# One scheduling context for both parts of a two-layer encoder trunk, with the latents kept in SBUF

## The chip, the cores and the metric

The kernel runs on one core of a Trainium2 chip. The metric is the device time of one execution in microseconds. The five engines are named as in the profile: PE (TensorE, with PEld for its weight loads), DVE (VectorE), ACT (ScalarE), POOL (GpSimd) and SP (SyncE, which here only issues DMAs). All numbers are 32 bit; each large matrix product is made of three matmuls over operands that are split into a high part and a low part.

## The reference

1024 tokens of width 1024 get 16 learned meta tokens in front (1040 in all) and pass two layers. The first is a gated linear attention, the second a latent attention whose keys and values come from a compressed latent. What matters here is the seam between them:

```python
# layer A ends:  h = x + (rms_norm(o) * silu(gate)) @ w_out
c = rms_norm(h, g) @ w_down                      # 256 latent + 64 rotary columns
c_kv = rms_norm(c[..., :256], g_latent)          # "ckv"
k_nope, v = c_kv @ w_uk, c_kv @ w_uv             # 8 heads x 128 each
# layer B, queries and gate:
z = rms_norm(h, g_b) @ w_in
c_q = rms_norm(z[..., :384], g_q_latent)         # "cq"
gate = z[..., 384:]                              # 1024 columns
q = rms_norm(c_q @ w_uq)                         # 8 heads x (128 + 64 rotary)
o = attention(q, k, v) * silu(gate)              # causal by chunks of 64
out = h + o @ w_out
```

## The kernel before, in words

`kernel` opens two tile contexts, one after the other, and each is scheduled by itself. `body` (L117) makes layer A, then the latents and the gates of layer B; `body2` (L961) makes the attention and the last projection. Within a context the scheduler orders the instructions of each engine by a simulation, and each engine then runs its own list in that order. The first context is planned by the plainer of two simulations, the second by the more detailed one. The engines all finish the first context before the second one starts.

The end of `body`: `latent_kv` (L878) and `latent_q` (L906) make the latents tile by tile in SBUF, transposed and split (`ckvT`, `cqT`), with the rotary key `kpe`, the sums `ssk` and the tables `qC`, `qS`. L934 to L938 write all of these to DRAM: the two latents on POOL's queue, the rest on SP's. Then the loop at L943 makes the gates, head by head: `load_wg` (L830) loads 512 KB of weights through SP and splits them (high part on POOL at L101, low part on DVE at L102); 48 matmuls fill two PSUM banks; ACT applies SiLU; SP stores the head's rows to DRAM (`gb_scr`, L954). The first head's weights (`wg0`) have a place of their own, so they are ready early; the others take turns in two buffers, which lie where the latents' weights `wd_hi` to `wq_lo` were.

The start of `body2`: POOL makes an identity matrix. `pair_weights(0, ...)` (L985) loads the up-projection weights of the first two heads (`uk`, `uv`, `uq`) and splits them, the high part on ACT (L1000) and the low part on DVE (L1001). `load(0, 1)` reads the first 256 tokens' latents (with the meta tokens) back from DRAM on POOL's queue, and SP reads the small tables. Constants such as `hide` and `qr_lo` are set on DVE. Then `build` makes one unit: keys, values and queries of 256 tokens for a pair of heads. Its first matmuls are the `uk` projection of `ckvT` (written to a bank of the tag `bd`), whose copy `kk` is squared on ACT, scaled on DVE, turned on PE, split again and used by `scores`. The remaining latents come with `load(1, NU)` (L1409).

The main loop (L1411) goes over 4 pairs of heads and 4 units each; `weave` mixes the scores of one unit with the build of the next and the weighing of the last. When the last unit is built, the pool `lcT` (latents and pair weights) is closed and the output weights `wf_hi`, `wf_lo` take its place (L1427 to L1438); `out_b` (L1443) then makes the output rows.

The order of two pools matters below. In `body` the PSUM pool `psB` (L752) has five banks for the tag `sc`, from which the gates take theirs in turn; in `body2` the pool `psB2` (L972) begins with the three banks of `bd`.

Of the kernel before, what the change touches and what calls it, by code (L numbers as in the profile page):

```python
# [28 lines left out]
NT = T // P  # L29
# [7 lines left out]
ROPE = 64  # L37
QK = NOPE + ROPE
# [10 lines left out]
def tools(tc):  # L49

    nc = tc.nc
    V, A, G, TE = nc.vector, nc.scalar, nc.gpsimd, nc.tensor
    uid = next(PART)
    number = [0]

    def tpool(**k):
        return tc.tile_pool(reuse_waits="tile", **k)

    def nm(s):
        number[0] += 1  # L60
        return f"{s}_{uid}_{number[0]}"

    NOSYNC = mybir.DependencyInfo(mybir.DependencyClass.NoSync, mybir.DependencyReason.DATA)
    tab = {"set": None, "before": [], "now": []}

    def act(out_ap, in_ap, func, **kw):

        want = {AF.Exp: "le", AF.Ln: "le", AF.Silu: "silu"}.get(func)

        def behind(i, others):  # L70
            for o in others:
                tc.add_manual_dep(i.ins, o.name, NOSYNC, reason="table order")

        new = want is not None and want != tab["set"]
        if new:
            tab["set"] = want
            tab["before"], tab["now"] = tab["now"], []
            if want == "le":
                i = A.preload_act_table_set("natural_log_exp_and_others")
                behind(i, tab["before"])  # L80
                tab["before"] = [i.ins]
        i = A.activation(out_ap, in_ap, func, **kw)  # L82
        if want is not None:
            behind(i, tab["before"])
            tab["now"].append(i.ins)
            if new and want != "le":
                tab["before"] = [i.ins]
        return i

    def mm3(ps, ahi, alo, bhi, blo, first, last):  # L90
        TE.matmul(ps, ahi, bhi, start=first, stop=False)  # L91
        TE.matmul(ps, ahi, blo, start=False, stop=False)  # L92
        TE.matmul(ps, alo, bhi, start=False, stop=last)  # L93

    def split_w(raw, hi, lo, gain=None, eng=G):

        if gain is None:
            eng.tensor_scalar(out=hi, in0=raw, scalar1=1.0, scalar2=1.0, op0=ALU.mult, op1=ALU.mult)  # L98
            V.tensor_tensor(out=lo, in0=raw, in1=hi, op=ALU.subtract)  # L99
        else:  # L100
            G.tensor_scalar(out=hi, in0=raw, scalar1=gain, scalar2=1.0, op0=ALU.mult, op1=ALU.mult)  # L101
            return V.scalar_tensor_tensor(out=lo, in0=raw, scalar=gain, in1=hi, op0=ALU.mult, op1=ALU.subtract)  # L102

    def split_ps(ps, hi, lo, gain=None):

        if gain is None:
            A.copy(hi, ps)  # L107
            V.tensor_tensor(out=lo, in0=ps, in1=hi, op=ALU.subtract)  # L108
        else:
            A.mul(hi, ps, gain)  # L110
            V.scalar_tensor_tensor(out=lo, in0=ps, scalar=gain, in1=hi, op0=ALU.mult, op1=ALU.subtract)

    return tpool, nm, act, mm3, split_w, split_ps


@with_exitstack
def body(ctx: ExitStack, tc: tile.TileContext, I):  # L117

    nc = tc.nc
    V, A, G, TE, SY = nc.vector, nc.scalar, nc.gpsimd, nc.tensor, nc.sync  # L120
    tpool, nm, act, mm3, split_w, split_ps = tools(tc)
# [14 lines left out]
    cp = ctx.enter_context(tpool(name="const", bufs=1))  # L136
# [612 lines left out]
        gathered = {t: out_gather(t, bank) for t in (-1, 0)}  # L749


    ps_b = ctx.enter_context(tpool(name="psB", bufs=2, space=PSUM))  # L752

    def bank2(tag, shape):
        tag = {"mm": "sc", "tr": "bd", "tb": "pt"}.get(tag, tag)
# [2 lines left out]
    with ExitStack() as lb:  # L758
# [172 lines left out]
                    wg0 = load_wg(lpre.enter_context(tpool(name="wg0", bufs=1, side="right")), 0)  # L931


        st = {}  # L934
        for key, y in (("ckvT", ckvT), ("cqT", cqT), ("kpe", kpe), ("ssk", ssk), ("qC", qC), ("qS", qS), ("gg", gg)):
            st[key] = nc.dram_tensor(key + "_scr", y.shape, F32R if "T" in key else F32).ap()
            (G if "T" in key else SY).dma_start(st[key], y)
        st.update(gb_scr=gb_scr, ot_scr=ot_scr, x1_scr=x1_scr)  # L938


        with ExitStack() as lg:
            wg = lg.enter_context(tpool(name="wg", bufs=2))
            for h in range(H):  # L943
                hi, lo = wg0 if h == 0 else load_wg(wg, h)
                z = wg.tile([P, T], F32, tag="z", name=nm("z"))
                for half in range(2):
                    c = slice(512 * half, 512 * half + 512)
                    cc = slice(NM + 512 * half, NM + 512 * half + 512)
                    ps = bank2("mm", [P, 512])
                    for kt in range(KT):  # L950
                        mm3(ps, hi[:, kt, :], lo[:, kt, :], h1_hi[:, kt, cc], h1_lo[:, kt, cc],
                            kt == 0, kt == KT - 1)
                    act(z[:, c], ps, AF.Silu)
                SY.dma_start(gb_scr[h * P:(h + 1) * P, :], z)  # L954
        lpre.close()

    return st


@with_exitstack  # L960
def body2(ctx: ExitStack, tc: tile.TileContext, I, out, st):  # L961

    nc = tc.nc
    V, A, G, TE, SY = nc.vector, nc.scalar, nc.gpsimd, nc.tensor, nc.sync
    tpool, nm, act, mm3, split_w, split_ps = tools(tc)

    cp = ctx.enter_context(tpool(name="const2", bufs=1))
    ident = cp.tile([P, P], F32, name="ident2")
    make_identity(nc, ident)
    gg = cp.tile([P, 1], F32, name="gg2")  # L970
    gb_scr, ot_scr, x1_scr = st["gb_scr"], st["ot_scr"], st["x1_scr"]
# [5 lines left out]
    lcT = ctx.enter_context(ExitStack())  # L977
    cpool = lcT.enter_context(tpool(name="cT2", bufs=1))

    wt = lcT.enter_context(tpool(name="wt", bufs=1))  # L980
    w_uk = I["kv_w_uk"].rearrange("(kt p) c -> p kt c", p=P)
    w_uv = I["kv_w_uv"].rearrange("(kt p) c -> p kt c", p=P)
    w_uq = I["b_w_uq"][0].rearrange("(kt p) c -> p kt c", p=P)

    def pair_weights(p, out_):  # L985

        h0 = 2 * p
        srcs = ((w_uk[:, :, h0 * P:(h0 + 2) * P], 2, 256, "uk"), (w_uv[:, :, h0 * P:(h0 + 2) * P], 2, 256, "uv"),
                (w_uq[:, :, h0 * QK:(h0 + 2) * QK], 3, 2 * QK, "uq"))
        raws = []  # L990

        for src, kts, w, _ in srcs:
            raws.append(wt.tile([P, 3, 2 * QK], F32, tag="raw", name=nm("raw"), bufs=3)[:, 0:kts, 0:w])
            SY.dma_start(raws[-1], src)
        yield 300
        for i, (_, kts, w, tag) in enumerate(srcs):
            hi = wt.tile([P, kts, w], F32R, tag=tag + "h", name=nm(tag))
            lo = wt.tile([P, kts, w], F32R, tag=tag + "l", name=nm(tag))
            if p == 0:
                A.copy(hi, raws[i])  # L1000
                V.tensor_tensor(out=lo, in0=raws[i], in1=hi, op=ALU.subtract)  # L1001
            else:
                split_w(raws[i], hi, lo)
            out_ += [hi, lo]
            yield 300

    wts = {0: []}
    w0 = pair_weights(0, wts[0])
    next(w0)
    ckvT = cpool.tile([P, 2, 2, L], F32R, name="ckvT2")  # L1010
    cqT = cpool.tile([P, 2, 3, T], F32R, name="cqT2")
    ckvT_hi, ckvT_lo, cqT_hi, cqT_lo = ckvT[:, 0], ckvT[:, 1], cqT[:, 0], cqT[:, 1]
    kpe = cpool.tile([P, NT + 1, ROPE], F32, name="kpe2")
    ssk = cpool.tile([P, NT + 1], F32, name="ssk2")
    qC, qS = (cpool.tile([P, NT, ROPE], F32, name=x) for x in ("qC2", "qS2"))

    def load(u0, u1):

        a, b = (0 if u0 == 0 else NM + 256 * u0), NM + 256 * u1
        four = lambda x: x.rearrange("p y j n -> p (y j) n")  # L1020
        G.dma_start(four(ckvT)[:, :, a:b], four(st["ckvT"])[:, :, a:b])
        a, b = 256 * u0, 256 * u1
        G.dma_start(four(cqT)[:, :, a:b], four(st["cqT"])[:, :, a:b])

    load(0, 1)
    for x, y in ((ssk, "ssk"), (kpe, "kpe"), (gg, "gg"), (qC, "qC"), (qS, "qS")):
        SY.dma_start(x, st[y])
    for _ in w0:
        pass


    lf = ctx.enter_context(ExitStack())
    with ExitStack() as lt:
# [372 lines left out]
        bd_t = lambda g: 7300 + (2000 if g == 0 else 0)  # L1406

        weave((started(0), 1, 0, 1))
        load(1, NU)  # L1409
        last, lt_ = None, 1  # L1410
        for n, (p, g) in enumerate(seq):  # L1411
            us = [units[p, u] for u in range(g + 1)]
# [88 lines left out]
```

## Time and profile before

| what | value |
|---|---|
| median of 3 runs | 1375.03 us (1369.99 to 1378.83) |
| profiled execution, its own time | 1379.86 us |
| its span, first to last instruction | 1378.0 us |
| mean granted TensorE clock | 0.978 |
| PE busy | 1320.7 us (96%) |
| DVE, ACT, POOL busy | 901.3, 541.7, 411.8 us |

The profile covers one execution. Its span is 1.86 us shorter than its device time, and its device time is 4.83 us above the median of the runs. A term that is read from the trace is taken off that execution, and the same difference is then taken off the median. A granted clock of 1.00 means 2.4 GHz and 0.50 means 1.2 GHz. Idle time of an engine is written in brackets in a timeline row, with what ended it.

### The profile page before, as it was taken

What the parts mean: (1) busy time and instruction counts of PE and PEld (TensorE: products, weight loads), DVE (VectorE), ACT (ScalarE), POOL (GpSimd) and SP (SyncE); (2) the same over time, 40 slices, a digit from 0 to 9 for tenths busy, and PEclk for the clock granted to TensorE, in tenths of its full rate; (3) what the DMA queues carried; (4) which work ended last, traced back from release to release, by engine and by line L of the source; (5) the groups of instructions that cost most, each with busy time, mean ns of one, the idle gap of its engine ahead of it and who ended that gap; (6) DMA issues with size and microseconds to landing.
All of it is one profiled execution on the core that took longest, in us unless ns stands there. A gap on an engine that the chain in (4) does not pass through costs nothing. (4 is left out here: it accounts for less than half of the span.)

```text
span 1378.0 us, 25002 instructions
## 1 busy us (share of the span) xinstructions
PE 1320.7 (96%) x9064; PEld 1191.2 (86%) x9064; DVE 901.3 (65%) x2625; ACT 541.7 (39%) x1709; POOL 411.8 (30%) x689
## 2 busy tenths in 40 slices
PE   6999999999999999999999999995999999998998
PEld 4879989988997999897788798884899999998787
DVE  5669778968986895544554764214887878878321
ACT  6442333233323431211222243114777777776200
POOL 3344224314332130041011402212454545347100
PEclk9999999999998999999999999997999999999999
DMA  5211202121211213136542306318010101004443
GB/s 175 46 25 47 51 20 65 32 50 40 53 42 24 54 39 92 51 96 222 166 141 79 108 1 224 108 46 265 25 49 28 61 24 33 24 32 135 129 147 118
DMA packets 121276, 109.01 MB, mean 79 GB/s; under 512 B 29230, under 2 KB 108142, under 8 KB 120898
## 3 DMA queue, kind: packets, MB, share of 16 engines
q1 hardware_dynamic: 118242, 96.88, 23.6%
q0 software_dynamic: 2912, 10.55, 2.1%
q8 instruction: 71, 1.16, 0.4%
q14 instruction: 51, 0.42, 0.1%
HBM read 74.29 MB, written 33.11 MB: 78 GB/s over the span
## 5 line engine op out<-in xcount | busy, mean ns | idle before, releaser
L91 PE MATMUL mm<-hT_hi,whi 128*128 128x384 f32 (+1 forms) x768 | 258.8, 337 | 2.6 <-DVE whi L98 2.5
L93 PE MATMUL mm<-hT_hi,wlo 128*128 128x384 f32 (+1 forms) x768 | 257.5, 335 | 0.4 <-DVE wlo L99 0.4
L92 PE MATMUL mm<-hT_lo,whi 128*128 128x384 f32 (+1 forms) x768 | 256.8, 334 | 0.0
L91 PEld LDWEIGHTS mm<-hT_hi,whi 128*128 128x128 f32 x768 | 148.4, 193 | 4.4 <-issue 3.2
L93 PEld LDWEIGHTS mm<-hT_hi,wlo 128*128 128x128 f32 x768 | 148.3, 193 | 3.2 <-DVE wlo L99 0.9
L92 PEld LDWEIGHTS mm<-hT_lo,whi 128*128 128x128 f32 x768 | 148.5, 193 | 1.3 <-issue 0.8
L108 DVE TENSOR_TENSOR pTl<-pt,pTh 128x256 fp32r<-128x256 f32 (+2 forms) x112 | 55.0, 494 | 14.1 <-ACT pTh L107 12.7
L98 POOL TENSOR_SCALAR whi<-raw 128x512 fp32r<-128x512 f32 x48 | 39.0, 826 | 73.6 <-PE mm L92 66.8
L82 ACT ACTIVATE P<-P,mx 128x144 f32<-128x144 f32 (+3 forms) x64 | 50.6, 791 | 21.2 <-DVE mx L1298 13.2
L91 PE MATMUL sc<-wo_hi,oTh 128*128 128x512 f32 (+1 forms) x144 | 57.5, 399 | 0.6 <-issue 0.6
L371 ACT COPY z<-mm 128x384 f32<-128x384 f32 (+1 forms) x72 | 31.9, 443 | 65.0 <-PE mm L93 64.8
L93 PE MATMUL sc<-wo_hi,oTl 128*128 128x512 f32 (+1 forms) x144 | 57.2, 397 | 0.0
L92 PE MATMUL sc<-wo_lo,oTh 128*128 128x512 f32 (+1 forms) x144 | 56.9, 395 | 0.0
L376 DVE SCALAR_TENSOR_TENSOR kn<-z,pcol,kn 128x384 f32<-128x384 f32 (+1 forms) x72 | 42.4, 589 | 18.3 <-POOL kn L373 17.4
L99 DVE TENSOR_TENSOR wlo<-raw,whi 128x512 fp32r<-128x512 f32 x64 | 47.3, 745 | 10.7 <-POOL whi L98 10.4
L102 DVE SCALAR_TENSOR_TENSOR wlo<-raw,pcol,whi 128x128 fp32r<-128x128 f32 x64 | 23.2, 419 | 46.2 <-POOL whi L101 46.2
L107 ACT CAST pTh<-pt 128x256 fp32r<-128x256 f32 (+2 forms) x112 | 47.2, 427 | 12.5 <-DVE pTl L108 8.6
L1311 POOL TENSOR_SCALAR P<-P,sl 128x144 f32<-128x144 f32 (+3 forms) x64 | 49.8, 778 | 4.2
L1309 POOL TENSOR_SCALAR Pe<-P,sl 128x128 f32<-128x128 f32 x64 | 27.1, 423 | 80.2 <-DVE sl L1306 55.1
L93 PE MATMUL sc<-h_hi,wlo 128*128 128x512 f32 x128 | 50.8, 397 | 0.0
L91 PE MATMUL bd<-wf_hi,oTh 128*128 128x512 f32 x128 | 50.0, 390 | 0.9 <-ACT oTh L1451 0.9
L91 PE MATMUL sc<-kn_hi,qn_hi 128*128 128x272 f32 (+3 forms) x160 | 48.4, 304 | 2.4 <-DVE mx L1298 1.9
(390 smaller groups left out, 4005.4 us busy)
## 6 DMA issues: line engine op xcount, KB each, us to landing
raw<-in_a_w_in SPq DMA_DIRECT2D x64, 256.0 KB
xt<-in_x SPq DMA_DIRECT2D x16, 512.0 KB
o_scr<-o SPq DMA_DIRECT2D x64, 64.0 KB
raw<-in_a_w_out SPq DMA_DIRECT2D x8, 512.0 KB
on<-o_scr SPq DMA_DIRECT2D x8, 512.0 KB
x_scr<-xt SPq DMA_DIRECT2D x8, 512.0 KB
raw<-in_b_w_in SPq DMA_DIRECT2D x8, 512.0 KB
gb_scr<-z SPq DMA_DIRECT2D x8, 512.0 KB
```

The lines of the kernel that those rows point to most:

```text
L82: i = A.activation(out_ap, in_ap, func, **kw)
L91: TE.matmul(ps, ahi, bhi, start=first, stop=False)
L92: TE.matmul(ps, ahi, blo, start=False, stop=False)
L93: TE.matmul(ps, alo, bhi, start=False, stop=last)
L98: eng.tensor_scalar(out=hi, in0=raw, scalar1=1.0, scalar2=1.0, op0=ALU.mult, op1=ALU.mult)
L99: V.tensor_tensor(out=lo, in0=raw, in1=hi, op=ALU.subtract)
L107: A.copy(hi, ps)
L108: V.tensor_tensor(out=lo, in0=ps, in1=hi, op=ALU.subtract)
L371: A.copy(z[:, 3 + a:3 + b], gemm_T(hi, lo, c))
L376: V.scalar_tensor_tensor(out=yc, in0=z[:, a + j:b + j], scalar=col("cw", 24 * j + m), in1=yc, op0=ALU.mult, op1=ALU.add)
L1309: G.tensor_scalar(out=Pe, in0=Pm[:, None, 0:NM].broadcast_to([P, E8, NM]), scalar1=s, scalar2=1.0, op0=ALU.mult, op1=ALU.mult)
L1311: G.tensor_scalar(out=Pm[:, 0:n], in0=Pm[:, 0:n], scalar1=s, scalar2=1.0, op0=ALU.mult, op1=ALU.mult)
```

## The change

There is one context. `body` goes on into what was `body2`, which becomes a block of it: a block is scheduled as a unit, nothing traced before it is placed among its instructions, and it is planned by the detailed simulation while the rest keeps the plain one. The latents, `kpe`, `ssk`, `qC`, `qS` and `gg` are not written to DRAM and read back; the attention reads the tiles that the latents were made in. The second identity matrix goes. The first pair's weights get tiles in a pool `wt` that is opened ahead of the gates, in the place right behind the latents; their loads are issued ahead of the gates' loop, and one step of their split is taken after the gate of each head from the third on, on POOL and DVE (it was ACT and DVE). The raw tiles have a size of their own for each of the three weights, where three of the largest size took turns.

```diff
-        st = {}
-        for key, y in (("ckvT", ckvT), ("cqT", cqT), ("kpe", kpe), ("ssk", ssk), ("qC", qC), ("qS", qS), ("gg", gg)):
-            st[key] = nc.dram_tensor(key + "_scr", y.shape, F32R if "T" in key else F32).ap()
-            (G if "T" in key else SY).dma_start(st[key], y)
+        wt = lcT.enter_context(tpool(name="wt", bufs=1))
...
+        wtiles = {}
+        for kts, w, tag in ((2, 256, "uk"), (2, 256, "uv"), (3, 2 * QK, "uq")):
+            wtiles[tag] = [wt.tile([P, kts, w], dt, name=tag + y) for y, dt in (("r", F32), ("h", F32R), ("l", F32R))]
+        def pair_weights(p, out_):
...
+            for src, kts, w, tag in srcs:
+                SY.dma_start(wtiles[tag][0], src)
+            yield 300
+            for i, (_, kts, w, tag) in enumerate(srcs):
+                raw, hi, lo = wtiles[tag]
+                split_w(raw, hi, lo)
+                out_ += [hi, lo]
+                yield 300
+        wts = {0: []}
+        w0 = pair_weights(0, wts[0])
+        next(w0)
...
                 SY.dma_start(gb_scr[h * P:(h + 1) * P, :], z)
+                if h > 1:
+                    next(w0, None)
         lpre.close()
-    return st
-def body2(ctx: ExitStack, tc: tile.TileContext, I, out, st):
...
-    ident = cp.tile([P, P], F32, name="ident2")
-    make_identity(nc, ident)
+    lps.close()
+    ctx.enter_context(tc.block(schedule_with_timeline_sim=True))
...
-            if p == 0:
-                A.copy(hi, raws[i])
-                V.tensor_tensor(out=lo, in0=raws[i], in1=hi, op=ALU.subtract)
-            else:
-                split_w(raws[i], hi, lo)
...
-        G.dma_start(four(ckvT)[:, :, a:b], four(st["ckvT"])[:, :, a:b])
...
-        G.dma_start(four(cqT)[:, :, a:b], four(st["cqT"])[:, :, a:b])
-    load(0, 1)
-    for x, y in ((ssk, "ssk"), (kpe, "kpe"), (gg, "gg"), (qC, "qC"), (qS, "qS")):
-        SY.dma_start(x, st[y])
...
-        load(1, NU)
...
-    with tile.TileContext(nc) as tc:
-        st = body(tc, I)
-    with tile.TileContext(nc, schedule_with_timeline_sim=True) as tc:
-        body2(tc, I, out, st)
+    with tile.TileContext(nc, schedule_with_timeline_sim=False) as tc:
+        body(tc, I, out)
```

## Rows read from the trace of the kernel before

**Rows 1.** Page, busy time, share of the span and instructions of each engine.

```profile
PE 1320.7 (96%) x9064; PEld 1191.2 (86%) x9064; DVE 901.3 (65%) x2625; ACT 541.7 (39%) x1709; POOL 411.8 (30%) x689
```

**Rows 2.** Stretches: length, busy us (instructions) of PE, PEld, DVE, ACT, POOL, clock, DMA.

```profile
920.00:930.00 10.00, 10.00 (x45) 8.06 (x44) 0.00 (x0) 1.20 (x2) 0.00 (x0) 1.00 0.13 52
...
931.70:945.10 13.40, 0.01 (x2) 0.04 (x1) 3.85 (x14) 3.45 (x5) 3.70 (x6) 0.67 0.78 217
945.00:955.00 10.00, 8.83 (x49) 7.91 (x49) 5.53 (x16) 6.63 (x25) 1.02 (x4) 0.75 1.17 373
955.00:965.00 10.00, 7.77 (x42) 6.51 (x43) 5.35 (x18) 5.34 (x19) 2.70 (x7) 0.83 0.74 252
```

**Rows 3.** Timeline of the seam: start us, us, engine, line, operation, idle before.

```profile
931.32 0.39 PE L93 MATMUL sc<-h_hi,wlo 128*128 128x512 f32 x1
931.74 0.60 ACT L82 ACTIVATE z<-sc 128x512 f32<-128x512 f32 x1 [4.94 <-PE sc L93]
...
936.07 0.20 POOL masks.py:197 MEMSET ident<- 128x128 f32 x1 [23.91 <-POOLq L1495]
...
936.08 1.28 ACT L79 ACT_TABLE_LOAD   x1 [3.74 <-PEq L1495]
...
936.54 0.82 POOL L1021 DMA_DIRECT2D ckvT<-ckvT_scr  x1 [0.26 <-issue]
...
936.93 1.65 DVE L1051 CAST qr_lo<-zero 64x256 fp32r<-64x256 f32 x4
...
944.77 1.15 ACT L1000 CAST uq<-raw 128x1152 fp32r<-128x1152 f32 x1 [4.13 <-DMA raw<-in_b_w_uq]
...
945.09 0.55 PE L91 MATMUL bd<-uk,ckvT 128*128 128x256 f32 x1 [13.39 <-DMA ckvT<-ckvT_scr]
```

**Rows 4.** Chain that ended last, in order of time, at the seam.

```profile
936.54 8.42 DMA ckvT<-ckvT_scr
```

**Rows 5.** Stretches, PE alone: length, PE busy, granted clock, DMA share, GB/s.

```profile
946.00:950.00 4.00, 4.00 (x21) 0.51 1.19 372
950.00:951.00 1.00, 1.00 (x10) 1.00 1.15 384
...
955.00:956.00 1.00, 0.00 (x0) 1.00 1.15 385
...
957.00:958.00 1.00, 1.00 (x5) 0.50 1.10 377
```

**Rows 6.** Timelines of PE and ACT, the first unit's build.

```profile
948.03 0.59 ACT L1153 COPY kk<-bd 128x512 f32<-128x512 f32 x1 [2.11 <-PE bd L93]
...
954.15 0.63 PE L1134 MATMUL bd<-ident,kk 128*128 128x128 f32 x4 [0.85 <-DVE v_lo L108]
956.05 0.26 PE L1134 MATMUL bd<-ident,kk 16*128 16x16 f32 x2 [1.27 <-DVE kk L1167]
...
959.10 0.48 ACT L1203 COPY qraw<-bd 128x384 f32<-128x384 f32 x1 [2.56 <-PE bd L93]
...
962.09 0.34 PE L91 MATMUL sc<-kn_hi,qn_hi 128*128 128x144 f32 x1 [0.48 <-ACT qn_hi L110]
```

**Rows 7.** Timelines of PE, POOL and ACT where the gates begin.

```profile
841.18 0.34 PE L93 MATMUL sc<-wq_hi,h_lo 128*128 128x384 f32 x1
...
853.35 0.60 ACT L82 ACTIVATE z<-sc 128x512 f32<-128x512 f32 x1 [4.74 <-PE sc L93]
...
875.58 2.99 POOL L101 TENSOR_SCALAR whi<-raw,pcol 128x128 fp32r<-128x128 f32 x8 [8.21 <-PE sc L92]
```

**Rows 8.** Load of the output weights: a stretch, POOL's groups, and a piece of the chain.

```profile
1270.00:1280.00 10.00, 7.28 (x54) 6.22 (x52) 6.58 (x16) 6.54 (x12) 6.96 (x7) 1.00 0.55 171
...
L1436 POOL TENSOR_TENSOR wf_lo<-raw,wf_hi 128x1024 fp32r<-128x1024 f32 x4 | 10.5, 2624 | 2.2 <-ACT wf_hi L1435 2.2
...
L98 POOL TENSOR_SCALAR wf_hi<-raw 128x1024 fp32r<-128x1024 f32 x4 | 4.2, 1049 | 1.4 <-DMA raw<-in_b_w_out 1.4
...
1266.69 3.56 DMA raw<-in_b_w_out
```

More of the change, by code (lines that the diff above doesn't have):

```diff
@@ L116, in body @@
 @with_exitstack
-def body(ctx: ExitStack, tc: tile.TileContext, I):
+def body(ctx: ExitStack, tc: tile.TileContext, I, out):
     nc = tc.nc
@@ L749, in body @@
         gathered = {t: out_gather(t, bank) for t in (-1, 0)}
-    ps_b = ctx.enter_context(tpool(name="psB", bufs=2, space=PSUM))
+    lps = ExitStack()
+    ps_b = lps.enter_context(tpool(name="psB", bufs=2, space=PSUM))
     def bank2(tag, shape):
@@ L931, in body @@
                     wg0 = load_wg(lpre.enter_context(tpool(name="wg0", bufs=1, side="right")), 0)
-        st = {}
-        for key, y in (("ckvT", ckvT), ("cqT", cqT), ("kpe", kpe), ("ssk", ssk), ("qC", qC), ("qS", qS), ("gg", gg)):
-            st[key] = nc.dram_tensor(key + "_scr", y.shape, F32R if "T" in key else F32).ap()
-            (G if "T" in key else SY).dma_start(st[key], y)
-        st.update(gb_scr=gb_scr, ot_scr=ot_scr, x1_scr=x1_scr)
+        wt = lcT.enter_context(tpool(name="wt", bufs=1))
+        w_uk = I["kv_w_uk"].rearrange("(kt p) c -> p kt c", p=P)
+        w_uv = I["kv_w_uv"].rearrange("(kt p) c -> p kt c", p=P)
+        w_uq = I["b_w_uq"][0].rearrange("(kt p) c -> p kt c", p=P)
+        wtiles = {}
+        for kts, w, tag in ((2, 256, "uk"), (2, 256, "uv"), (3, 2 * QK, "uq")):
+            wtiles[tag] = [wt.tile([P, kts, w], dt, name=tag + y) for y, dt in (("r", F32), ("h", F32R), ("l", F32R))]
+        def pair_weights(p, out_):
+            h0 = 2 * p
+            srcs = ((w_uk[:, :, h0 * P:(h0 + 2) * P], 2, 256, "uk"), (w_uv[:, :, h0 * P:(h0 + 2) * P], 2, 256, "uv"),
+                    (w_uq[:, :, h0 * QK:(h0 + 2) * QK], 3, 2 * QK, "uq"))
+            for src, kts, w, tag in srcs:
[9 more added lines that the diff above has]
+        next(w0)
         with ExitStack() as lg:
@@ L954, in body @@
                 SY.dma_start(gb_scr[h * P:(h + 1) * P, :], z)
+                if h > 1:
+                    next(w0, None)
         lpre.close()
-    return st
-@with_exitstack
-def body2(ctx: ExitStack, tc: tile.TileContext, I, out, st):
[L963 to L967, printed above, removed]
-    ident = cp.tile([P, P], F32, name="ident2")
-    make_identity(nc, ident)
-    gg = cp.tile([P, 1], F32, name="gg2")
-    gb_scr, ot_scr, x1_scr = st["gb_scr"], st["ot_scr"], st["x1_scr"]
+    lps.close()
+    ctx.enter_context(tc.block(schedule_with_timeline_sim=True))
     ps_b = ctx.enter_context(tpool(name="psB2", bufs=2, space=PSUM))
@@ L975, in bank2 @@
         return ps_b.tile(shape, F32, tag=tag, name=nm(tag), bufs={"sc": 2, "bd": 3, "pt": 2, "po": 1}[tag])
[L977 to L998, printed above, removed]
-            if p == 0:
-                A.copy(hi, raws[i])
-                V.tensor_tensor(out=lo, in0=raws[i], in1=hi, op=ALU.subtract)
-            else:
-                split_w(raws[i], hi, lo)
[L1004 to L1020, printed above, removed]
-        G.dma_start(four(ckvT)[:, :, a:b], four(st["ckvT"])[:, :, a:b])
-        a, b = 256 * u0, 256 * u1
-        G.dma_start(four(cqT)[:, :, a:b], four(st["cqT"])[:, :, a:b])
-    load(0, 1)
-    for x, y in ((ssk, "ssk"), (kpe, "kpe"), (gg, "gg"), (qC, "qC"), (qS, "qS")):
-        SY.dma_start(x, st[y])
-    for _ in w0:
-        pass
     lf = ctx.enter_context(ExitStack())
```

## Prediction, made before the changed kernel ran

> **What bounds the kernel now.** The page comes first: PE is busy 96% of the span [rows 1], so a change pays only where PE stands still or is slow, and the question is where the other 4% lie. The stretches show it: in the gates PE is busy 10.00 of 10.00 us, and then, where one context ends and the next begins, 0.01 of 13.40 us; the 20 us behind that give only 8.83 and 7.77 of 10 [rows 2]. The timeline says what the gap is made of. The last gate matmul starts at 931.32, the last SiLU runs from 931.74 to 932.34, then no engine computes until 936.07 (the end of the first context), POOL issues the first latent load at 936.54, and the first matmul of the attention starts at 945.09 after 13.39 us of idle, released by that load [rows 3]. The chain puts 8.42 us on the load [rows 4]. The other inputs were late too: the last of the first pair's weights, `uq`, is split on ACT only at 944.77 [rows 3]. The last view is the granted clock: right after the gap PE runs at 0.51 for 4 us, which is 1.2 GHz, goes to 1.00, stands still again, and is at 0.50 once more from 957 [rows 5].
>
> **The change part by part.** *The gap.* With the latents in SBUF, the pair weights split ahead and no second context, the first matmul of the attention waits only for PE's own queue and for a PSUM bank. The first tag of the new pool begins at the first bank. The five `sc` buffers were taken 51 times in turn (18 out-projections, 9 and 8 latents, 16 gate halves), so the last gate half is in buffer 0, the same bank: the first projection must wait for the last SiLU, which ends at 932.34 [rows 3]. It could start as early as 931.7 if the slot fell elsewhere. I take 932.4, as counted: 945.09 - 932.4 = 12.7 us saved (13.4 at most).
>
> *Entry of the block.* Nothing in the trace shows a block. The nearest rows are an issue gap of 0.26 us and the whole end of a context, 932.34 to 936.07, 3.73 us [rows 3]. No drain of stores is asked for here, so I take 0.3, near the lower end, and keep 3.7 for a rival. Below nothing is excluded: entering cannot give time.
>
> *The clock behind the gap.* With 0.7 us of idle in place of 13.4 the clock should still be at 1.00, as it is through the gates [rows 2]. The slow stretch delayed the copy `kk`, which came 2.94 us after the first matmul (945.09 to 948.03) [rows 3, 6]. The twelve matmuls ahead of it take half as long at 2.4 GHz; with the part that is not PE's clock left out, I put the saving at 1.2 us, between 0 and 1.47 (half of 2.94). Behind the copy, the slow matmuls ran beside ACT's squares, and saving there brings nothing forward. The second slow stretch (957 to 960, the second query) delayed `qraw` at 959.10 and costs up to 1.5 us, half of three such rows. It came after PE had stood idle for 0.85 and 1.27 us behind DVE's scaling of the keys [rows 5, 6]. That wait is still there and, with the projections faster, longer. I take 0 and keep 1.5. The Trainium skill (TensorE: Matmul & The Clock Gate, on HAM oscillation) says that idle PE time brings the throttle back each time anew; by it the second stretch stays, which is also the value taken.
>
> *Work that lay in the gap.* The splits of the first pair on ACT and DVE, the identity matrix and about ten loads leave it, and they were all off the path except `uq` and the latents. The splits go under the gates on POOL and DVE, where POOL has 2.99 us of work and then 8.21 us of idle for each head [rows 7]: the cover is ample, cost 0. Without that cover they would cost a few us once. DVE's constants (`qr_lo`, 1.65 us [rows 3], and some shorter ones) lie over the gates' input and must now wait for the last gate matmul. The build first needs DVE behind its matmuls, the copy of 0.59 us [rows 6] and four squares on ACT, so they fit; each us that they were longer than that would cost one. The table load of 1.28 us on ACT [rows 3] fits between the SiLU and the copy.
>
> *Queues.* POOL's stores and loads of the latents go, four loads among them at 0.82 us of issue [rows 3]; POOL had nothing urgent behind the stores. On SP the pair loads stand ahead of the gates' weights and wait for the latents' first weights alone. More serious: the gates' two weight buffers now lie over the query weights, whose last matmul is at 841.18. The load for head 1 can start no earlier. With 3.56 us for a load of the same 512 KB [rows 8] and 2.99 us of splits it is ready at about 848, and PE needs it when head 0 is done, shortly before that head's second SiLU starts at 853.35 [rows 7]. Margin 4 to 5 us, cost 0. If the cover goes, the excess is paid once.
>
> *The order of the attention.* The planner starts from another state, so the lists of all engines may differ. Bounds: what PE stands idle in the first 20 us, 1.17 + 2.23 = 3.4 us [rows 2], could vanish, or come twice, and the 2.72 us of idle beside the load of the output weights [rows 8] could come twice: -3.4 to +6.1. I take 0, since the same planner arranges the same work.
>
> *Sum.* -12.7 + 0.3 - 1.2 = -13.6 us. The profiled execution of 1379.86 goes to 1366.3, and the median of 1375.03 to 1361.4. About 1% (13.75 us) is what a measurement of this kernel can tell from no change, so the forecast sits on that bound.
>
> **The rivals.** *More comes back*: the second slow stretch goes as well (1.5) and half the idle of the first 20 us (1.7). For it: inputs that arrive late shaped that order. Against: the chain of copy, squares, scaling and turning is ACT's and DVE's [rows 6]. -16.8 us, 1358.2; with the free bank, no entry cost and all the idle, 1355.5.
>
> *The entry costs what the end of a context costs.* If each engine must finish and branch, 3.7 us in place of 0.3, and with that idle time the clock's 1.2 may be lost: -10.2 to -9.0 us, about 1365.4. For it: 3.73 us in which nothing ran [rows 3]. Against: in that time the last store had to land, which no one need wait for now. The Trainium skill (Runtime: NRT & Kernel Launch, Instruction fetch mechanics) says that a taken branch whose target is not loaded stalls the engine until it is fetched; no run here shows it. By that rule the entry costs something on every engine, and this rival is how it would look.
>
> *The order gets worse*, +6.1 us: 1367.5. For it: DVE and POOL are dense where the output weights are loaded. Against: nothing in the dependencies has changed there.
>
> *The output weights come after the attention.* Their place is that of pools that are opened outside the block and closed in it. If it is only free when all the attention has run, the load no longer hides: POOL's part alone is 10.5 + 4.2 = 14.7 us and the first load 3.56 [rows 8], so -13.6 + 18.3 = +4.7 us, 1379.7, slower than before. It decides at one point: whether the first `wf_hi` split comes before the last scores. Against: the tiles waited on are the latents and pair weights, done with the last query.
>
> **How the numbers follow.** The forecast has 0.40, with its own range 1359.5 to 1363.5; more comes back 0.22; the entry 0.18; a worse order 0.12; the load behind the attention 0.08. The range 1355.5 to 1369 holds the first three and most of the fourth. Faster by over 1% is below 1361.3: nearly all of the second case and half of the forecast, 0.41. Slower by over 1% is above 1388.8, beyond every case worked out: 0.03, for two bad cases together. The rest, 0.56, is within 1%.
>
> **What the changed profile would show.** Right: the idle time ahead of the first `bd` matmul is about 0.7 us and ends with ACT's SiLU; the clock is 1.00 in the 4 us behind it; `kk` follows that matmul by some 1.8 us; the gates are as dense as before, with `uk`, `uv`, `uq` split under them; the time from the first `bd` matmul to the end is some 1 us shorter than before (1378.0 - 945.09 = 432.9). Wrong: an idle of several us ahead of the first projection with no engine at work (entry); a stop at the second gate head (buffers); a stretch of the attention that is longer by several us (order); the output weights' split behind the last scores. A latents stage that has another order than before, which I count at nothing, would also make it wrong.

## The result, and the profile after

The changed kernel took 1359.03 us (median of 4 runs, 1355.85 to 1360.76), the kernel before beside it 1374.01 us: a ratio of 0.988, 95% interval 0.9845 to 0.9915, that is 11.7 to 21.3 us less. The forecast was 1361.4 us, the range 1355.5 to 1369.0. The profiled execution took 1358.79 us with a span of 1357.1 us, against 1379.86 and 1378.0 before.

The page first, engines' busy time, share of the span and instructions, which answers to [rows 1]:

```profile
PE 1313.5 (97%) x9064; PEld 1184.5 (87%) x9064; DVE 905.6 (67%) x2625; ACT 537.2 (40%) x1706; POOL 408.7 (30%) x684
```

PE has the same 9064 matmuls and is busy for 7.2 us less, although the span is 20.9 us shorter. Two things therefore happened: idle time went, and matmuls ran at a higher clock. The timeline of the seam, PE and ACT, answers to [rows 3] and to the copy in [rows 6]:

```profile
925.12 0.39 PE L93 MATMUL sc<-h_hi,wlo 128*128 128x512 f32 x1
925.54 0.60 ACT L82 ACTIVATE z<-sc 128x512 f32<-128x512 f32 x1 [4.94 <-PE sc L93]
926.16 1.28 ACT L79 ACT_TABLE_LOAD   x1
926.19 0.38 PE L91 MATMUL bd<-ukh,ckvT 128*128 128x256 f32 x1 [0.69 <-ACT z L82]
927.95 0.59 ACT L1111 COPY kk<-bd 128x512 f32<-128x512 f32 x1 [0.51 <-issue]
...
934.75 0.63 PE L1092 MATMUL bd<-ident,kk 128*128 128x128 f32 x4 [2.48 <-DVE kk L1125]
...
940.50 0.34 PE L91 MATMUL sc<-kn_hi,qn_hi 128*128 128x144 f32 x1 [0.20 <-ACT qn_hi L110]
```

The brackets are to be read first: the idle time ahead of the first projection is 0.69 us in place of 13.39, and its releaser is the last SiLU. The copy `kk` follows that projection by 927.95 - 926.19 = 1.76 us (2.94 before). Further on, PE waits 2.48 us for DVE's scaling of the keys where it waited 0.85, and the first scores come 14.31 us behind the first projection (17.00 before). The stretches of that time, which answer to [rows 2, 5], columns as there:

```profile
915.00:925.00 10.00, 10.00 (x45) 8.07 (x44) 0.00 (x0) 0.60 (x1) 0.00 (x0) 1.00 0.13 52
925.50:926.20 0.70, 0.01 (x2) 0.01 (x1) 0.00 (x0) 0.64 (x2) 0.00 (x0) 1.00 0.00 0
926.00:930.00 4.00, 3.81 (x32) 3.68 (x33) 0.00 (x0) 3.38 (x11) 0.00 (x0) 1.00 0.71 222
930.00:940.00 10.00, 6.44 (x39) 5.00 (x38) 6.24 (x23) 6.57 (x28) 3.74 (x8) 1.00 0.30 102
940.00:944.00 4.00, 3.80 (x17) 3.53 (x18) 2.59 (x8) 1.86 (x6) 0.79 (x2) 0.60 0.01 4
```

The clock stays at 1.00 behind the seam, and is lost once, at 940 to 944, after ten microseconds in which PE was busy for 6.44.

From the end of the last gate matmul to the end of the program there are now 431.59 us (446.29 before): -14.7. The other 6.2 us of the 20.9 lie ahead of the seam. PE's list up to there is the old one but for 82 of its 6092 places, all of them in the latents' stage, and that stage takes as long as it did (70.3 us over its last 405 matmuls before, 70.6 after). So the 6.2 us lie further ahead, and the stretches show where, PE alone, columns as in [rows 5]; first the kernel before:

```profile
420.00:424.00 4.00, 4.00 (x17) 0.61 0.29 74
424.00:428.00 4.00, 4.00 (x22) 0.50 0.01 2
428.00:432.00 4.00, 4.00 (x24) 0.50 0.10 16
432.00:436.00 4.00, 4.00 (x21) 0.68 0.12 21
```

and the changed one:

```profile
420.00:424.00 4.00, 4.00 (x31) 1.00 0.28 74
424.00:428.00 4.00, 4.00 (x36) 1.00 0.13 22
428.00:432.00 4.00, 3.93 (x51) 1.00 0.10 16
432.00:436.00 4.00, 4.00 (x71) 1.00 0.08 23
```

In that execution of the kernel before, the clock was at its lower level for 13.7 of these 16 us (from 420.9 to 434.5), with less than half as many matmuls in them. Whether this belongs to the change is the first question put to the chip.

### The profile page after: what moved, and what is told of

Same layout as the page of the kernel before. It is cut to its first block, busy times and chain, and to the rows that moved or that the text cites. A ratio compares the mean times of both kernels' runs of the same rounds, so it can differ in the third digit from the quotient of the medians.

```text
span 1357.1 us, 24958 instructions
## 1 busy us (share of the span) xinstructions
PE 1313.5 (97%) x9064; PEld 1184.5 (87%) x9064; DVE 905.6 (67%) x2625; ACT 537.2 (40%) x1706; POOL 408.7 (30%) x684
## 4 chain that ended last, share of the span: by engine, by line
PE 76%; DVE 8%; POOL 6%; ACT 4%; DMA 3%; issue 2%; SPq 0%; DVEq 0%; POOLq 0%; ACTq 0%
PE mm L93 7%; PE mm L91 7%; PE mm L92 7%; PE sc L93 6%; PE sc L92 6%; PE sc L91 6%; PE bd L91 4%; PE bd L92 4%; PE bd L93 4%; PE pt L1298 2%; PE tr L484 1%; PE ch L599 1%; PE ch L595 1%; ACT junk L82 1%; PE ch L609 1%
## 5 line engine op out<-in xcount | busy, mean ns | idle before, releaser
L82 ACT ACTIVATE P<-P,mx 128x144 f32<-128x144 f32 (+3 forms) x64 | 50.6, 791 | 21.3 <-DVE mx L1256 18.7
L375 DVE SCALAR_TENSOR_TENSOR kn<-z,pcol,kn 128x384 f32<-128x384 f32 (+1 forms) x72 | 42.3, 589 | 17.4 <-POOL kn L372 16.5
L92 PE MATMUL sc<-h_lo,whi 128*128 128x512 f32 x128 | 50.6, 396 | 0.0
L91 PE MATMUL sc<-h_hi,whi 128*128 128x512 f32 x128 | 50.5, 395 | 0.0
```

Of the source, the lines that this page charges most:

```text
L375: V.scalar_tensor_tensor(out=yc, in0=z[:, a + j:b + j], scalar=col("cw", 24 * j + m), in1=yc, op0=ALU.mult, op1=ALU.add)
```

## The experiments

**Theory A**: the gain is the seam's idle time and what the clock loses with it, and it comes from the one context, in which loads and engines can go on past the last gate. **Rivals**: the gain is the DRAM trip of the latents that is saved; it is the weights made early; it is the block and its finer order; a part of it is the clock elsewhere. The runs came in three groups, each with runs of the kernel before on the same chip (medians 1374.15, 1374.78 and 1372.28 us).

All profiles are read in the same way here: from the end of the last gate matmul to the first score matmul (the seam and the first unit's build), and from there to the end. The two kernels that were profiled twice differ from themselves by 1 to 3 us in each of the next columns, so no smaller difference between two rows counts.

| kernel | last gate ends | idle ahead of the first projection | to the first scores | from there to the end | time, ratio to before |
|---|---|---|---|---|---|
| before | 931.71 | 13.39 | 30.38 | 415.91 | 1374.01 |
| before, again | 923.07 | 13.99 | 29.38 | 419.15 | 1378.2, 1.0023 |
| changed | 925.51 | 0.69 | 14.99 | 416.60 | 1359.03, 0.988 |
| changed, again | 924.75 | 0.69 | 16.47 | 417.68 | 1357.65, 0.9871 |
| own first bank | 920.30 | none | 14.49 | 418.81 | 1358.34, 0.9882 |
| barrier | 923.82 | 0.69 | 16.00 | 418.68 | 1360.12, 0.9901 |
| latents by DRAM | 929.52 | 0.69 | 15.91 | 416.87 | 1362.18, 0.991 |
| weights in the block | 919.12 | 5.54 | 22.23 | 417.85 | 1365.18, 0.9932 |
| latents late | 926.83 | 10.06 | 26.98 | 419.89 | 1369.56, 0.9974 |
| no block | 924.82 | 0.69 | 17.01 | 464.07 | 1405.17, 1.022 |

**The kernel before, again (`same_before`).** Nothing edited.

> The kernel before, unchanged, run again. The profiles of before and after differ by 20.9 us of span, but 6.2 us of that lie ahead of the seam: the last gate ends at 931.7 and at 925.5, and in the first of the two the clock was at half for 13 us around 424 to 436, in a stretch where both kernels run the same list of PE instructions. Theory A (chance of the clock): the same program gives gate ends that differ by some us from profile to profile; here the last gate ends anywhere from 925 to 932, the idle behind it is again 13.4 us, and the median is within 0.4% of before. Theory B (the change moved something ahead of the seam): the last gate ends again at 931 to 932 here and near 925.5 in every variant of after.

Measured: 1378.2 us, ratio to itself 1.0023 (1.0002 to 1.0045). In its profile the last gate ends 8.6 us sooner than in the first one of the same program. The same stretches as above:

```profile
420.00:424.00 4.00, 4.00 (x42) 3.19 (x41) 2.22 (x12) 1.97 (x13) 0.49 (x1) 1.00 0.04 10
424.00:428.00 4.00, 4.00 (x30) 3.31 (x29) 3.33 (x15) 1.13 (x4) 0.30 (x1) 1.00 0.23 37
428.00:432.00 4.00, 3.93 (x51) 3.04 (x49) 3.10 (x11) 1.37 (x4) 2.14 (x5) 1.00 0.06 16
```

The slow stretch is not there (clock, third column from the right). It is there again, 13.7 us long, in the profiles of `latents_by_dram`, `latents_late` and `no_block`, which run the changed kernel's list in that stretch. So it wasn't the change that took it away. Up to the last gate the clock is at its lower level for 41.0 us in the first profile of this kernel and for 23.9 in the second; half of the difference is 8.5 of the 8.6 us. The last gate, expected at 925 to 932, ends at 923.07 here, and over the table anywhere in 12.6 us, so two single profiles can't be subtracted from end to end. The seam itself repeats: idle 13.39 and 13.99.

**The changed kernel, again (`same_after`).** Nothing edited.

> The changed kernel once more, unaltered. Theory A (what the change is worth is fixed; what moves its profiled execution is the clock ahead of the seam): last gate's end anywhere in 918 to 930 us, but idle at the seam 0.69 us again, and from the last gate's end to the end of the program 432 us plus or minus 2.5 (the same kernel before gave 446.7 and 448.9). Ratio to the kernel before 0.985 to 0.992. Rival (the profile of the changed kernel was a lucky one): 436 us or more behind the last gate, ratio 0.993 or more.

Measured: 1357.65 us, ratio 0.9871 (0.9846 to 0.9897), idle 0.69 us, 434.15 us behind the last gate. Theory A as expected, at the very edge of its 2.5 us: the expectation counts from the start of the last gate matmul, 0.39 us sooner, which gives 434.5 against 432.

**The first projection gets a bank of its own (`own_first_bank`).**

```diff
+    ps_t = lps.enter_context(tpool(name="psT", bufs=2, space=PSUM))
     ps_b = lps.enter_context(tpool(name="psB", bufs=2, space=PSUM))
...
-        return ps_b.tile(shape, F32, tag=tag, ...)
+        return (ps_b if tag == "sc" else ps_t).tile(shape, F32, tag=tag, ...)
```

> The first projection of the attention gets a PSUM bank that the gates don't use, so TensorE no longer waits for the last SiLU; its order of instructions is that of the changed kernel. Theory A (entering the block costs TensorE nothing, the 0.69 us are the SiLU's alone): idle falls from 0.69 to 0.1 us or less, the copy of kk, which is behind SiLU and table load on ScalarE, moves at most 0.6 us, the end by 0 to 0.6 us; ratio to the kernel before as the changed kernel within 0.1%. Rival (the entry has a price of its own that the SiLU hid): idle of 0.3 to 0.7 us stays, and nothing moves.

Measured: 0.9882 (0.9853 to 0.9911), as the changed kernel. The timeline of PE and ACT at its seam:

```profile
919.90 0.40 PE L93 MATMUL sc<-h_hi,wlo 128*128 128x512 f32 x1
920.13 0.28 PE L91 MATMUL bd<-ukh,ckvT 128*128 128x256 f32 x1
...
920.33 0.60 ACT L82 ACTIVATE z<-sc 128x512 f32<-128x512 f32 x1 [4.95 <-PE sc L93]
920.95 1.28 ACT L79 ACT_TABLE_LOAD   x1
922.24 0.59 ACT L1112 COPY kk<-bd 128x512 f32<-128x512 f32 x1
```

No bracket stands at the first projection: it is issued 0.23 us behind the last gate matmul, like any matmul behind another. So entering the block cost PE nothing that the trace can show, and the 0.69 us were the bank's. They bring nothing to the end: `kk` now comes right behind SiLU and table load on ACT, which, as I read it, is the chain that sets the pace.

**A barrier ahead of the block (`barrier`).** One line, `tc.strict_bb_all_engine_barrier()`, ahead of the block.

> After, with a barrier of all engines between the gates and the block, so that no engine starts the block before all have done all that comes ahead of it. This is what the rival of the prediction called the end of a context (3.73 us in before). Theory A: the last gate's store must land, which costs 2 to 4 us of idle time ahead of the first projection, +2 to +5 us with the clock, about 1362 to 1364. Rival (a barrier costs next to nothing and all of the gap was the loads): under 1 us, 1359.

Measured: 0.9901 (0.9872 to 0.9931); idle 0.69 us as without it, and the first scores 16.00 us behind the last gate. The rival's size came out, but not because a barrier is cheap. This line held nothing back where it was meant to: DVE sets its constants of the block 20 us ahead of PE's first projection at 924.51, as without the line.

```profile
904.73 0.48 DVE L1001 MEMSET hide<- 128x512 f32 x1
```

So the run says nothing on what a barrier costs.

**The latents by DRAM, inside the one context (`latents_by_dram`).** They are stored to scratch and loaded into the same tiles again.

```diff
+            st[key] = nc.dram_tensor(key + "_scr", y.shape, F32R).ap()
+            G.dma_start(st[key], y)
...
     ctx.enter_context(tc.block(schedule_with_timeline_sim=True))
+    load(0, 1)
```

> After, but both latents are written to DRAM behind the latents' stage, and read back into the same tiles in the block, in the two steps of before; weights stay early, one context stays. Theory A: the seam is again as long as that load, 8.4 us plus its issue, with the clock at half behind it: idle of 8 to 11 us ahead of the first projection, +9 to +12 us against after, about 1369. Rival (the end of a context was the larger part, the load is short when no weights come with it): +3 to +5 us, about 1363.

Measured: 0.991 (0.9876 to 0.9943), idle 0.69 us. Both expectations missed, since the load wasn't exposed. POOL's timeline:

```profile
906.99 2.98 POOL L101 TENSOR_SCALAR whi<-raw,pcol 128x128 fp32r<-128x128 f32 x8 [8.22 <-PE sc L92]
909.92 0.82 POOL L970 DMA_DIRECT2D ckvT<-ckvT_scr  x1
910.75 0.83 POOL L972 DMA_DIRECT2D cqT<-cqT_scr  x1
```

POOL was done with the gates at 909.97 and went on into the block's list, 20 us ahead of PE. The load ran under the last two gate heads, and landed 4.2 us after its issue. The median is near the rival's 1363, but its wait isn't there, and the time behind the last gate, 432.78 us, lies between the changed kernel's two (431.59 and 434.15). Keeping the latents on chip is thus not what the gain rests on: in one context the round trip costs nothing that these runs can tell.

**The same, with the reload held back (`latents_late`).**

```diff
+            G.tensor_copy(ckvT[0:1, 0, 0, 0:1], z[0:1, T - 1:T])
```

behind the last gate head, on top of `latents_by_dram`.

> As the one with the latents by DRAM inside the one context, and GpSimd copies one element of the last gate (which the reload overwrites) into the latents' tile ahead of the reloads, so that they can't be issued before the last SiLU. Theory A (of the 13.39 us at the seam before, the exposed reload is the larger part, and the context's end of 3.7 us the smaller; the one context gains because the reload can go out under the gates): SiLU 0.6, copy 0.3, issue to landing 8.4 as before, so idle of 9 to 10 us, released by the reload; last gate's end to the end 439 to 442 us, ratio 0.992 to 0.996. Rival (the reload was long only because a new context starts all queues afresh): idle of 5 us or less, 432 to 436 us behind the last gate.

Measured: 0.9974 (0.9942 to 1.0006). Nearly all of the gain is gone (the interval takes in 1), though there is still one context. POOL's and PE's timelines:

```profile
927.52 0.18 POOL L990 CAST ckvT<-z 1x1 fp32r<-1x1 f32 x1 [20.25 <-ACT z L82]
928.00 0.83 POOL L970 DMA_DIRECT2D ckvT<-ckvT_scr  x1 [0.30 <-POOL ckvT L990]
...
936.89 0.55 PE L91 MATMUL bd<-ukh,ckvT 128*128 128x256 f32 x1 [10.06 <-issue]
```

From issue to first matmul there are 8.89 us, as with the load of [rows 4] (8.42). The idle is just above theory A's band, but the size expected behind it was too low: 446.87 us behind the last gate against 439 to 442 (the ratio's interval still takes in the expected 0.992 to 0.996). Two terms had been left out. From inside the gap the clock is at its lower level until 941.4, so the first 4.5 us of matmuls run at it (0.73 in the second row is the mean of that and of 1.00 behind it, columns as in [rows 2]):

```profile
926.00:937.00 11.00, 0.94 (x5) 0.49 (x3) 0.22 (x1) 1.88 (x2) 3.40 (x5) 0.73 0.85 222
937.00:945.00 8.00, 7.95 (x45) 7.21 (x45) 2.02 (x8) 4.39 (x21) 0.00 (x0) 0.73 1.18 403
```

so that projection to scores took 16.92 us (14.31 and 15.79 in the changed kernel); and the attention behind the first scores took 419.89, the longest of the table but for `no_block`. The seam and first build took 29.4 to 30.4 us before, take 27.0 with an exposed reload, and 15.0 to 16.5 in the changed kernel. So an exposed load with its slow clock is enough for some 11 us of the gain. The other 3 I put down to the end of the context (3.74 us of idle on ACT in [rows 3]); that is argued, not shown, for before the change the first pair's weights were late too.

**The first pair's weights in the block (`weights_in_block`).** They are loaded and split at the head of the block, in place of under the gates.

```diff
-        w0 = pair_weights(0, wts[0])
-        next(w0)
...
-                if h > 1:
-                    next(w0, None)
...
     ctx.enter_context(tc.block(schedule_with_timeline_sim=True))
+    for _ in pair_weights(0, wts[0]):
+        pass
```

> After, but the first pair's weights are loaded and split in the block instead of under the gates. Theory A (the seam is what its last input makes it): the load lands some 3.2 us after its issue and the split of uk takes 0.62 and 0.69 us, so the first projection starts about 5 us after the last SiLU instead of 0.05: +5 us against after, perhaps 1.2 more if the clock falls in that idle time; about 1364 to 1365. Rival (the latents alone were the gain, the weights hide): within 1 us of after, 1359.

Measured: 0.9932 (0.9906 to 0.9958), 7 to 8 us above the changed kernel by the ratios (0.9932 against 0.988 and 0.9871). Timelines of SP, POOL and PE:

```profile
908.59 11.51 SPq L974 DMA_DIRECT2D gb_scr<-z  x2
920.19 0.39 SPq L950 DMA_DIRECT2D ukr<-in_kv_w_uk  x1
...
923.99 0.62 POOL L98 TENSOR_SCALAR ukh<-ukr 128x512 fp32r<-128x512 f32 x1 [24.42 <-DMA ukr<-in_kv_w_uk]
...
924.66 0.80 PE L91 MATMUL bd<-ukh,ckvT 128*128 128x256 f32 x2 [5.54 <-POOL ukh L98]
```

SP stands at the store of the last gate, which waits for the last SiLU, and the weights' load is queued behind it (the 11.51 us hold two stores; the longest wait of SP's queue for a SiLU there is 10.9 us). The first projection starts 4.90 us behind the last SiLU, as theory A had it. It is the mirror image of POOL's case: an engine whose list ends early enters the block early, one that waits for the last result doesn't. The early weights are worth 6 to 7 us of seam here (22.23 against 15.0 to 16.5): 4.85 are idle (5.54 against 0.69), and 0.9 to 2.4 lie between projection and scores, where the clock is 0.54 and 0.61 over eight microseconds.

**No block, one plain order (`no_block`).** The block's line is taken out; the attention is then ordered like the rest, without `schedule_with_timeline_sim`. Up to the last gate PE's order is unchanged but for two matmuls that change places.

> One scheduling context without the block: the attention is ordered by the same plain simulation as the rest, everything up to the last gate is in the order of the changed kernel. Theory A (what matters is the one context, not the block or the finer simulation): idle at the seam 0.69 us again, last gate's end to the end within -3.4 and +6.1 of the changed kernel's 432 us (the bounds of the prediction for an order), so 429 to 438, total at most 6 us over the changed kernel. Rival (the finer order carries part of the gain): 440 us or more behind the last gate, ratio to the kernel before over 0.995.

Measured: 1405.17 us, 1.022 (1.0186 to 1.0254): slower than before. The seam is as good (idle 0.69), and the attention 47 us longer. PE's groups between 926 and 1300, name, count, busy us and mean ns, idle before and releaser, of this kernel:

```profile
L91 PE MATMUL sc<-kn_hi,qn_hi 128*128 128x272 f32 (+3 forms) x160 | 50.7, 317 | 12.5 <-DVE mx L1255 12.4
L1297 PE MATMUL pt<-ident,P 128*128 128x128 f32 x272 | 45.1, 284 | 11.8 <-DVE pm L1289 9.6 <-DVE pTl L108 2.3
```

and of the changed one:

```profile
L91 PE MATMUL sc<-kn_hi,qn_hi 128*128 128x272 f32 (+3 forms) x160 | 48.2, 303 | 1.0 <-DVE mx L1256 0.8 <-ACT qn_hi L110 0.2
L1298 PE MATMUL pt<-ident,P 128*128 128x128 f32 x288 | 46.3, 276 | 3.2 <-POOL P L1269 1.5 <-DVE pTl L108 0.8 <-DVE pm L1290 0.7
```

These two groups wait 24.3 us, all of it for DVE's maxima and products, in place of 4.2. PE as a whole is busy for 336.1 of the 374 us of that window, and for 362.2 in the changed kernel, so 26 us more of it are idle. Theory A was wrong here, and the -3.4 to +6.1 us that the prediction gave an order are no bound for another way of ordering.

**The whole program in the finer order (`fine_whole`).** No block, and `schedule_with_timeline_sim=True` for everything.

> No block, and the whole program in the finer simulation's order, ahead of the latents too. With the plain simulation for the attention the program took 1405 us, 481 us of them behind the last gate. Theory A (it is the finer order that the attention needs, not the block): 430 to 436 us behind the last gate; the part ahead changes by an unknown amount, within 10 us either way. Rival (the block's own boundary, which keeps gates and attention apart, makes the order): 445 us or more behind the last gate.

Measured: 1496.03 us, 1.0886 (1.084 to 1.0932). PE's timeline at the seam:

```profile
1065.88 0.38 PE L91 MATMUL bd<-ukh,ckvT 128*128 128x256 f32 x1 [0.69 <-ACT z L82]
```

From there to the end of the span (1497.1) there are 431.2 us, as in the changed kernel (430.91). So it is the finer order and not the block's boundary that the attention needs; but up to there the same order costs some 140 us, far beyond the 10 expected. The clock is part of it: it is at its lower level for 198 us up to the last gate, 27 in the changed kernel, which by an estimate (half the difference) is some 85 of the 140. The block is what lets each part keep its own.

**The first unit's projections under the last gate head.** They were tried in two forms. First without a block (`early_unit`, to be held against `no_block`); it also has the bank of its own, one gate buffer `z` in place of two and an earlier end of `wdr`, for room.

```diff
+                    if h == H - 1:
+                        if half == 0:
+                            early_keys(None, P, 2, 0)
+                            early_keys(None, NM, 1, -1)
+                        else:
+                            early_query(0)
+                            early_query(1)
```

> As the one without a block, but the first unit's key projections, their copy and squares, and its two query projections with copies, squares and rotation are put under the last head's gate: TensorE has the gate's matmuls to fill the waits of that ramp. In the changed kernel TensorE is idle for 4.5 us between 925.5 and 942, and the slow clock of 938 to 946 costs 1.7 us more. Theory A (the ramp is what is still late at the seam, and what it gives is kept): 4 to 6 us less than the one without a block from the first gate's matmul to the end. Rival (given back: behind the ramp the attention is held by the order of its units, as 2.0 of the 2.7 us that the ramp became shorter were kept): 0 to 2 us less. Third possibility (the moved work delays the last SiLUs and copies on ScalarE): 1 to 3 us more.

Measured: 1407.78 us, 1.0236 (1.021 to 1.0261). From the first gate matmul to the end its profile has 567.71 us, `no_block` 571.41, 3.7 less; the times don't show it. Inconclusive. Then with the block, the early results in raw weight tiles that are free by then (`early_block`; the bank of its own is in it too).

> The changed kernel with its block and finer order, and the first unit's key projections, copies, squares, and both query projections with copies, squares and rotation put under the last head's gate; they live in the raw weight tiles of the first pair, which are free by then. Theory A (the ramp is what is still late, and what it gives is kept): the first scores come 3 to 5 us sooner behind the first gate's matmul than the changed kernel's 105.3 and 106.8 us (two profiles; some 4 us of projections are among them and stay), and the end with them, 3 to 5 us under the changed kernel: 1353 to 1355 us. Rival (given back by the order of the units): the first scores come sooner, and the end by 0 to 1.5 us. Third (the raw weights of the second pair, which now wait for the first unit, come late): a new wait at the second pair, 0 to 3 us slower.

Measured: 1358.88 us, 0.9901 (0.9865 to 0.9937): no gain over the changed kernel. From the first gate matmul the first scores come after 104.07 us (105.32 and 106.83 in the changed kernel), the end after 523.65 (521.92 and 524.51). Its stretches, columns as in [rows 2]:

```profile
925.00:930.00 5.00, 4.48 (x29) 3.83 (x27) 0.18 (x2) 2.58 (x9) 0.00 (x0) 1.00 0.26 92
930.00:935.00 5.00, 2.21 (x11) 1.78 (x12) 4.42 (x20) 2.09 (x7) 0.00 (x0) 0.70 0.36 118
935.00:940.00 5.00, 4.65 (x21) 4.25 (x21) 2.44 (x5) 1.98 (x5) 0.79 (x2) 0.50 0.50 172
940.00:945.00 5.00, 5.00 (x33) 5.00 (x31) 1.64 (x8) 3.83 (x15) 0.76 (x2) 0.78 0.00 1
```

The first scores come 1.3 to 2.8 us sooner, less than the 3 to 5 of theory A, and from them to the end it takes 419.58 us, 1.9 to 3.0 more than in the changed kernel: there the shorter build was paid back. With the projections gone from it PE has little to do between 930 and 935, while ACT and DVE finish the keys. The clock goes to 0.50, and over the 15 us it loses 0.30 x 5 + 0.50 x 5 + 0.22 x 5 = 5.1 us worth of full speed, against 0.40 x 4 = 1.6 in the changed kernel's one slow stretch (3.4 in its second profile, summed in the same way). This sum is an upper bound, since it counts time in which PE stood idle and a low clock costs nothing. Behind the first scores the clock is low for 5.8 us here (936.4 to 942.2) and for 3.4 in the changed kernel, and half of the difference is 1.2 us. So the clock can be a part of what was paid back; how much of the rest is the order of the units, as the rival had it, wasn't tested.

## Why the prediction was right, step by step

*The gap*, 12.7 us: measured 13.39 - 0.69 = 12.70, released by the last SiLU through the shared bank, as counted; `own_first_bank` shows that it was the bank. The second pair of profiles gives 13.3.

*The entry*, 0.3 us: 0, by `own_first_bank`. The rival that put the end of a context there (chance 0.18) falls. With it goes the rule of the Trainium skill (Runtime: NRT & Kernel Launch, Instruction fetch mechanics) as a cost here: PE shows no stall at the entry in that run, 0.23 us from the last gate matmul to the first projection. Whether there is a branch to code that was not loaded, no view shows.

*The clock behind the gap*, 1.2 us: `kk` at 1.76 in place of 2.94 us, so 1.18, in both pairs of profiles. From the first projection to the end it is 432.91 to 430.91 us in the first pair and 434.54 to 433.47 in the second, so 2.0 and 1.1 us, where some 1 was forecast.

*The second slow stretch*, taken as 0: it didn't go, it moved, from 957 to 960 [rows 5] to 940 to 944. In the changed kernel it follows the longer wait for DVE (2.48 us), which the prediction had named. It moves between executions of one program as well, and the place decides what it costs. Before the change it lies ahead of the first scores in one profile and behind them in the other (952.6 to 956.0), and they come 17.00 and 15.39 us after the first projection. After the change it lies behind them in the first profile and ahead of them in the second (935.5 to 938.9): 14.31 and 15.79 us. So some 1.5 us, the price that the prediction had put on it, were gained in the first pair of profiles and lost in the second by chance. The sentence of the Trainium skill on HAM oscillation (TensorE: Matmul & The Clock Gate) agrees with the trace in part (its own case is longer waits, for a DMA). The clock is 0.60 behind that idle time, 0.50 in `early_block`, 0.54 in `weights_in_block`, but in `own_first_bank` it stays at 1.00 for 16 us behind a wait of 2.92 us at the same place. Which wait brings it down isn't shown. So "more comes back" was the wrong mechanism. The time, 1359.0, came out nearer to its 1358.2 than to the forecast only because the kernel before was 1.0 us faster beside it; the saving, 15.0 us, is nearer to the forecast's 13.6 than to 16.8.

*Work that lay in the gap*: free under the gates, as said, and dear outside them, 7 to 8 us in `weights_in_block`. One step was wrong without a price: DVE's constants didn't wait for the last gate matmul at 925.12, they ran 17 us ahead of it.

```profile
907.34 1.19 DVE L1009 CAST qr_lo<-zero 64x256 fp32r<-64x256 f32 x4
```

*Queues.* The cover was mis-sized: a margin of 4 to 5 us was forecast for the second gate head. The pair's loads were to wait for the latents' first weights alone, but SP's queue stood at the first of them for 53.6 us until the last query matmul, and they went out right ahead of head 1's load:

```profile
835.40 0.38 SPq L950 DMA_DIRECT2D ukr<-in_kv_w_uk  x1
836.85 12.12 SPq L832 DMA_DIRECT2D raw<-in_b_w_in  x3
```

POOL's timeline where the gates begin answers to [rows 7]:

```profile
838.69 0.62 POOL L98 TENSOR_SCALAR ukh<-ukr 128x512 fp32r<-128x512 f32 x1 [54.17 <-PE bd L920]
839.27 0.62 POOL L98 TENSOR_SCALAR uvh<-uvr 128x512 fp32r<-128x512 f32 x1
842.66 1.16 POOL L98 TENSOR_SCALAR uqh<-uqr 128x1152 fp32r<-128x1152 f32 x1 [2.77 <-DMA uqr<-in_b_w_uq]
844.36 6.71 POOL L101 TENSOR_SCALAR whi<-raw,pcol 128x128 fp32r<-128x128 f32 x16 [0.55 <-DMA raw<-in_b_w_in]
```

POOL was held for 2.77 us by `uq`'s load, and began head 1's first piece only at 844.36; DVE began its low part at 845.48. PE began the gates at 835.18 and was at head 1 after 48 matmuls, at 846.26, where it needed the high part, and at 846.72 the low part: 1 to 2 us of margin. It was enough, PE is busy 4.00 of the 4.00 us from 844 and 7.00 of the 7.00 from 848.

*The order ahead of the seam*, counted at nothing: the latents' stage did get another order, the sign that the prediction named, but it cost nothing (70.3 and 70.5 us before, 70.6 and 70.4 after, over the 405 matmuls ahead of the gates).

*The order of the attention*, taken as 0: from the first scores to the end 415.91 and 419.15 us before, 416.60 and 417.68 after. The value holds; the bounds hold for this planner alone (`no_block`).

*The output weights after the attention* (chance 0.08): they didn't wait. POOL's first `wf_hi` split starts at 1235.26, ahead of the last scores at 1252.4, and the first output matmul follows at 1263.9.

*The sum*, -13.6 us: the two pairs of profiles give -14.7 and -14.4 behind the last gate, the medians -15.0 and, in the second group, -17.1. The intervals reach from -11.7 and from -14.2, so the forecast lies at the small end of the first and just outside the second. 1 to 3 us that the medians have beyond the measured terms (-12.7 and -1.2) are below what the spread ahead of the seam lets one place, and stay open. The medians came out on the faster side of the 1% bound, which had 0.41 against 0.56; the first group's interval reaches over that bound.

## What to carry to other kernels

The seam between two scheduling contexts cost here the latency that couldn't be started before it, so ask first what could be issued earlier if the boundary were gone. Even the round trip through DRAM cost nothing that could be told once its queue reached it under other work, and data on chip gained some 9 us in place of 15 to 17 when another load was queued behind the last result (`weights_in_block`). Merge contexts, but let each part keep the ordering it was good with. When work is taken out of a stretch where PE waits, look at the granted clock before the gain is counted.

## What was unexpected of the hardware

The same program, on the same inputs, had 13.7 us of low clock between 420 and 436 in one execution and none in another; the last gate ended at 931.71 and 923.07, and nearly all of that is the clock. And the low clock of a gap lasted longer than the gap: behind the seam in `latents_late`, 10.06 us of idle, the clock stayed at 0.50 for another 4.5 us of dense matmuls (4.9 and 5.3 in the two profiles of the kernel before), whose first took 0.55 us in place of 0.38.
